# One subtraction of each weight block pair goes from VectorE to GpSimd

## The chip, the cores and the metric

The kernel runs on 1 core of one Trainium2 chip. A core has a matrix engine, TensorE (PE in the profile; PEld is its weight load, which overlaps the matmuls), and three engines that work on tiles: VectorE (DVE), ScalarE (ACT) and GpSimd (POOL). SyncE (SP) issues the transfers from main memory here. Each engine takes its instructions in the program's order and waits for the others by semaphores. Tiles lie in SBUF, the results of matmuls in PSUM. The metric is the device time of one execution, in microseconds.

## The reference

Two layers of a small diffusion transformer work on 256 latent tokens and 256 context tokens of width 1024. Each layer has a swiglu, a mixer (a short convolution in the first layer, attention in the second) and another swiglu, each with a modulated norm ahead of it and a gate behind it:

```python
def _swiglu(h, w13, w2):
    gte, up = jnp.split(h @ w13, 2, axis=-1)
    return (jax.nn.silu(gte) * up) @ w2

for i in range(DEPTH):
    mod = (jax.nn.silu(c) @ mod_w[i] + mod_b[i]).reshape(bsz, 3, 3, 1, D_MODEL)
    lat = lat + 0.5 * mod[:, 0, 2] * _swiglu(_modulate(lat, ...), ffn_w13[i, 0], ffn_w2[i, 0])
    ...   # the same for the context, then the mixer, then the second swiglu
```

The hidden width is 2816, 22 blocks of 128. All of it is computed in float32.

## The kernel before

**Three matmuls for one.** A matmul here takes operands in a shortened form of float32 (F32R). To keep float32's precision, each operand is split into a high part, which is the operand rounded, and a low part, which is what the rounding left. `split` (L91) does that: ScalarE copies with rounding (L92), VectorE subtracts the copy from the source (L93). `mm3` (L112) then issues three matmuls: high by high (L116), high by low of the moving operand (L117), and low of the weight by high (L118). Every weight passes through `split` after it is loaded.

**Seven products for eight.** In most of the swiglus, where latent and context tokens are worked on together, a block of gate weights and its block of up weights are taken as a 2 x 2 arrangement of sub-blocks (A11, A12, A21, A22), and the inputs as another, and the product is formed in seven smaller products rather than eight. The class `Pair` (L525) does it for one of the 22 blocks. Its constructor loads the raw weights, 128 x 2048, forms the sums S1 to S4 on VectorE (L548, L554, L556), and splits A11 with A12, S1 with S2, and S3 with S4, in tiles of 1024 columns named wh and wl, with four buffers of each. A22 is split last, into tiles of 512 columns named w4h and w4l (L558 to L561), with two buffers of each. Raw blocks (wr) have three buffers; the queue of SyncE refills one (L88) when all that read it are done.

**The order within a pair.** The products are `head` (A11, A12), `five` (S1), `six` (S2, S4), `seven` (S3) and `four` (A22). The loop in `ffn` (L600) interleaves two pairs: `head` and `five` of a pair, `seven` of the pair before, `six` of this pair, `four` of the pair before. So A22's high and low parts are read later than any other block of their pair. Between the products VectorE joins sums (L586, L591), multiplies gate and up (L597) and subtracts for the low part of the result (gl, L93).

**Thirds.** A swiglu goes through its 22 blocks in thirds of 8, 7 and 7. After each third, `project` (L454) multiplies what was formed by the third's rows of the second weight matrix (tiles py) and adds it to the residual x (L438). The last two pairs' products are mixed into the beginning of that. The first swiglu starts differently: its first third mostly takes the plain form. The last swiglu works on the latent tokens alone and has no pairs. In all there are 56 pairs.

**What else VectorE does.** The modulation vectors of all layers come from products and sums of VectorE (tiles junk, L136), which are issued in small portions by `tick` during `project`. At the start of a swiglu the norm's steps stand there (t, bl and the sums of L323 to L328).

**What sets the order.** The kernel's text gives the instructions with priorities; a scheduler of the framework puts them in an order for each engine by its own estimates of their lengths. So moving one instruction may change the order of others. GpSimd is not used in the kernel's body.

Of the kernel before, what the change touches and what calls it, by code (L numbers as in the profile page):

```python
# [9 lines left out]
F32 = mybir.dt.float32  # L10
F32R = mybir.dt.float32r
BF16 = mybir.dt.bfloat16
AF = mybir.ActivationFunctionType
ALU = mybir.AluOpType
# [25 lines left out]
def hybrid_kernel(ctx: ExitStack, tc: tile.TileContext, a: dict, out: bass.AP):  # L40
    nc = tc.nc
# [12 lines left out]
    def nm(s):  # L54
        uid[0] += 1
        return f"{s}{uid[0]}"
# [29 lines left out]
    def load_raw(src, n=2048):  # L86
        raw = wp.tile([P, 2048], F32, name=nm("wr"), tag="wr", bufs=3)
        nc.sync.dma_start(raw[:, :n], src)  # L88
        return raw

    def split(hi, lo, src):  # L91
        nc.scalar.activation(out=hi, in_=src, func=AF.Copy)  # L92
        nc.vector.tensor_tensor(out=lo, in0=src, in1=hi.bitcast(F32), op=ALU.subtract)  # L93

    def half():

        return tuple(
            wp.tile([P, 1024], F32R, name=nm(t), tag=t, bufs=4) for t in ("wh", "wl")
        )
# [170 lines left out]
    class Plain:  # L270


        def __init__(self, w=T2):
            self.w, self.n = w, 1024 // w
            self.t = [(hot("hh"), hot("hl")) for _ in range(KT // self.n)]
# [249 lines left out]
    class Pair:  # L525
# [6 lines left out]
        def __init__(self, src, h):  # L532
            self.h = h
            raw = load_raw(src)
            a21, a22, a11, a12 = (raw[:, i * T2 : i * T2 + T2] for i in range(4))
            tt = nc.vector.tensor_tensor
            sm = wp.tile([P, 2048], F32, name=nm("ws"), tag="ws", bufs=1)
            s1, s2, s3, s4 = (sm[:, i * T2 : i * T2 + T2] for i in range(4))
            self.w = {}

            def keep(keys, src):
                hi, lo = half()
                split(hi, lo, src)
                for i, key in enumerate(keys):
                    self.w[key] = [t[:, i * T2 : i * T2 + T2] for t in (hi, lo)]

            keep(("A11", "A12"), raw[:, 1024:])
            tt(  # L548
                out=sm.rearrange("p (a b c) -> p a b c", a=2, b=2)[:, :, 0, :],
                in0=a21.unsqueeze(1).to_broadcast([P, 2, T2]),  # L550
                in1=raw[:, T2 : 3 * T2].rearrange("p (a c) -> p a c", a=2),
                op=ALU.subtract,
            )
            tt(out=s2, in0=a11, in1=s1, op=ALU.subtract)  # L554
            keep(("S1", "S2"), sm[:, :1024])
            tt(out=s4, in0=a12, in1=s2, op=ALU.subtract)  # L556
            keep(("S3", "S4"), sm[:, 1024:])
            self.w["A22"] = [  # L558
                wp.tile([P, T2], F32R, name=nm(t), tag=t, bufs=2) for t in ("w4h", "w4l")
            ]  # L560
            split(*self.w["A22"], a22)  # L561

        def prod(self, ps, wk, hk, first=True):
            for k in range(4):
# [143 lines left out]
    for s in range(2):  # L708
# [6 lines left out]
        out=sb1, in0=modb[:, 0, KT : 2 * KT], scalar1=1.0, scalar2=None, op0=ALU.add  # L715
# [96 lines left out]
    for m in range(KT):  # L812
# [4 lines left out]
        for c0, c1 in ((0, S), (S, T2)) if m == 0 else ((0, T2),):  # L817
# [15 lines left out]
            out=d, in0=u, scalar1=convk[:, 1, m : m + 1], scalar2=None, op0=ALU.mult  # L833
# [4 lines left out]
            out=d2[:, :, 1:], in0=u2[:, :, : S - 1], scalar=convk[:, 0, m : m + 1],  # L838
            in1=d2[:, :, 1:], op0=ALU.mult, op1=ALU.add,
        )  # L840
        nc.vector.scalar_tensor_tensor(
            out=d2[:, :, : S - 1], in0=u2[:, :, 1:], scalar=convk[:, 2, m : m + 1],
            in1=d2[:, :, : S - 1], op0=ALU.mult, op1=ALU.add,
# [151 lines left out]
    for kv in range(KVH):  # L995
# [7 lines left out]
        out=scq, in0=rq[:, :16], scalar1=float(P) ** -0.5, scalar2=None, op0=ALU.mult  # L1003
# [163 lines left out]
```

## Time and profile before

| | us |
|---|---|
| median of 3 runs | 1614.27 |
| lowest and highest | 1613.15, 1616.92 |
| profiled execution | 1611.37 |
| its span | 1609.5 |
| TensorE busy | 1576.1 |
| VectorE busy | 1332.4 |
| ScalarE busy | 722.2 |
| GpSimd busy | 0.2 |
| mean granted TensorE clock | 0.992 of full speed |

The span is from the first instruction's start to the last one's end; the profiled execution took 1.87 us more than its span. Matmuls overlap in their pipeline: a 256-column one is shown with some 283 ns, but the next starts 120 ns after it, so a busy TensorE may still lose time to waits, and starts are what to read. In a row of the timeline come start, length, engine, line, operation and tiles, and in brackets how long the engine stood idle before it and for whom. In a group's row, behind the bar, come busy time in us, mean length in ns, and the idle time before them. A row of waits has the total in us, the number and the longest. The chain of waits is followed back from the last instruction, at each step to what released it.

### The profile page before, as it was taken

To read this page: it belongs to the slowest core of one execution; us is meant where nothing else is said; L and a number is where in the kernel's file an instruction comes from. 1 tells how busy PE (TensorE), PEld (TensorE's weight loads), DVE (VectorE), ACT (ScalarE), POOL (GpSimd) and SP (SyncE) were. 2 spreads that over 40 slices of the span, in tenths; PEclk is the share of its full clock that TensorE was granted. 3 is DMA by queue.
4 is the path that set the end of the run, shared out by engine and by line. 5 is a ranking of instruction groups with operands and counts; after the bars stand their busy time and mean duration, and the time that the engine had idled before them with its cause. 6 is when DMAs were issued, how large, how long until landed. Compare 5 with 4: busy or idle time off the path is not lost.

```text
span 1609.5 us, 25613 instructions
## 1 busy us (share of the span) xinstructions
PE 1576.1 (98%) x10566; PEld 1450.1 (90%) x10566; DVE 1332.4 (83%) x2035; ACT 722.2 (45%) x1110; POOL 0.2 (0%) x4
## 2 busy tenths in 40 slices
PE   9999999999999999999999999999999999899999
PEld 6788998999888889899899889889899897789999
DVE  4988778879998889799797999898898789965554
ACT  5532452544322365335255465245254455454443
POOL 0000000000000000000000000000000000000000
PEclk9999999999999999999999999999999999999999
DMA  8456235234565513353433413452432463755453
GB/s 320 162 183 209 80 122 180 90 135 152 177 221 186 180 41 117 132 183 100 168 120 115 154 54 131 172 195 96 156 129 96 180 214 108 270 201 185 169 194 109
DMA packets 38277, 248.77 MB, mean 155 GB/s; under 512 B 5136, under 2 KB 6928, under 8 KB 12304
## 3 DMA queue, kind: packets, MB, share of 16 engines
q1 hardware_dynamic: 35712, 245.38, 43.7%
q10 hardware_dynamic: 2448, 1.76, 0.4%
q8 instruction: 82, 1.34, 0.3%
q14 instruction: 35, 0.29, 0.1%
HBM read 244.77 MB, written 1.05 MB: 153 GB/s over the span
## 4 chain that ended last, share of the span: by engine, by line
PE 82%; DVE 12%; DMA 3%; ACT 2%; issue 1%; DVEq 0%; ACTq 0%; SPq 0%
PE py L117 7%; PE py L116 7%; PE py L118 7%; PE p L116 6%; PE p L118 6%; PE p L117 6%; PE q L118 5%; PE q L116 5%; PE q L117 5%; DVE junk L136 4%; DVE wl L93 3%; PE pg L117 2%; PE pg L118 2%; PE pg L116 2%; PE pu L117 2%; PE pu L118 2%
## 5 line engine op out<-in xcount | busy, mean ns | idle before, releaser
L92 ACT ACTIVATE wh<-wr 128x1024 fp32r<-128x1024 f32 (+2 forms) x274 | 274.4, 1014 | 395.0 <-PE py L117 108.7
L93 DVE TENSOR_TENSOR wl<-wr,wh 128x1024 fp32r<-128x1024 f32 (+2 forms) x274 | 318.2, 1167 | 97.0 <-ACT wh L92 96.4
L136 DVE CUSTOM_DVE_ANT_0 junk<-wr,scbc,modb 128x1024 bf16<-128x1024 f32 x236 | 302.5, 1282 | 39.6 <-DMA wr<-in_modT 37.0
L117 PE MATMUL py<-gl,wh 128*128 128x512 f32 (+1 forms) x746 | 263.2, 353 | 0.0
L116 PE MATMUL py<-gh,wh 128*128 128x512 f32 (+1 forms) x746 | 263.1, 353 | 0.0
L118 PE MATMUL py<-gh,wl 128*128 128x512 f32 (+1 forms) x746 | 262.9, 352 | 0.0
L93 DVE TENSOR_TENSOR wl<-ws,wh 128x1024 fp32r<-128x1024 f32 x112 | 136.8, 1223 | 27.3 <-ACT wh L92 27.0
L118 PEld LDWEIGHTS py<-gh,wl 128*128 128x128 f32 x746 | 141.1, 189 | 19.1
L116 PEld LDWEIGHTS py<-gh,wh 128*128 128x128 f32 x746 | 141.2, 189 | 18.6
L117 PEld LDWEIGHTS py<-gl,wh 128*128 128x128 f32 x746 | 141.2, 189 | 18.0
L92 ACT ACTIVATE wh<-ws 128x1024 fp32r<-128x1024 f32 x112 | 117.8, 1057 | 76.4 <-PE p L117 34.2
L116 PE MATMUL p<-th,wh 128*128 128x256 f32 x448 | 126.8, 283 | 0.0
L117 PE MATMUL p<-tl,wh 128*128 128x256 f32 x448 | 126.8, 283 | 0.0
L118 PE MATMUL p<-th,wl 128*128 128x256 f32 x448 | 126.6, 283 | 0.0
L117 PE MATMUL q<-bl,wh 128*128 128x256 f32 x336 | 95.2, 283 | 0.0
L116 PE MATMUL q<-bh,wh 128*128 128x256 f32 x336 | 95.1, 283 | 0.0
L118 PE MATMUL q<-bh,wl 128*128 128x256 f32 x336 | 95.1, 283 | 0.0
L438 DVE SCALAR_TENSOR_TENSOR x<-py,G,x 128x256 f32<-128x256 f32 x168 | 74.2, 480 | 21.4 <-PE py L118 21.2
L116 PEld LDWEIGHTS p<-th,wh 128*128 128x128 f32 x448 | 86.0, 192 | 0.5 <-ACT sg L584 0.2
L117 PEld LDWEIGHTS p<-tl,wh 128*128 128x128 f32 x448 | 86.0, 192 | 0.3
L118 PEld LDWEIGHTS p<-th,wl 128*128 128x128 f32 x448 | 85.9, 192 | 0.0
L116 PE MATMUL pg<-hh,wh 128*128 128x256 f32 (+1 forms) x240 | 75.8, 316 | 4.6 <-ACT hh L260 4.6
(236 smaller groups left out, 4001.3 us busy)
## 6 DMA issues: line engine op xcount, KB each, us to landing
wr<-in_w SPq DMA_DIRECT2D x88, 1024.0 KB, 4.9
wr<-in_modT SPq DMA_DIRECT2D x67, 1024.0 KB, 4.9
wr<-in_w2b SPq DMA_DIRECT2D x32, 896.0 KB, 4.6
wr<-in_w2a SPq DMA_DIRECT2D x16, 1024.0 KB, 4.9
wr<-in_cw_cx SPq DMA_DIRECT2D x8, 1024.0 KB, 4.9
wr<-in_mod SPq DMA_DIRECT2D x5, 1024.0 KB, 7.4
wr<-in_cw_b SPq DMA_DIRECT2D x4, 1024.0 KB, 4.8
wr<-in_cw_out SPq DMA_DIRECT2D x4, 1024.0 KB, 4.9
```

Source lines behind the costliest of these rows:

```text
L92: nc.scalar.activation(out=hi, in_=src, func=AF.Copy)
L93: nc.vector.tensor_tensor(out=lo, in0=src, in1=hi.bitcast(F32), op=ALU.subtract)
L116: nc.tensor.matmul(ps, wh, mh, start=first, stop=False, **kw)
L117: nc.tensor.matmul(ps, wh, ml, start=False, stop=False, **kw)
L118: nc.tensor.matmul(ps, wl, mh, start=False, stop=last, **kw)
L136: nc.vector.tensor_tensor_reduce(out=junk, in0=raw[:, j * D : j * D + D], in1=scbc[:, v, :], scale=1.0, scalar=modb[:, l, col : col + 1], ...
L438: nc.vector.scalar_tensor_tensor(out=x[:, m, s * S : s * S + S], in0=ps[:, o : o + S], scalar=g[:, m, s : s + 1], in1=x[:, m, s * S : s * ...
```

## The change

In the constructor of `Pair`, the split of A22 is written out. ScalarE's rounding stays as it was. The subtraction that gives the low part w4l, 128 x 512, is issued to GpSimd instead of VectorE. Operands, tiles and buffers are the same; all 56 pairs are touched.

```diff
             self.w["A22"] = [
                 wp.tile([P, T2], F32R, name=nm(t), tag=t, bufs=2) for t in ("w4h", "w4l")
             ]
-            split(*self.w["A22"], a22)
+
+            hi, lo = self.w["A22"]
+            nc.scalar.activation(out=hi, in_=a22, func=AF.Copy)
+            nc.gpsimd.tensor_tensor(out=lo, in0=a22, in1=hi.bitcast(F32), op=ALU.subtract)
```

## The prediction

> **What bounds the kernel now.** I began with the page's busy times, went on to its chain of waits, and then cut the span into stages, because the change touches only the stages that work on block pairs.
>
> ```profile
> PE 1576.1 (98%) x10566; PEld 1450.1 (90%) x10566; DVE 1332.4 (83%) x2035; ACT 722.2 (45%) x1110; POOL 0.2 (0%) x4
> PE 82%; DVE 12%; DMA 3%; ACT 2%; issue 1%; DVEq 0%; ACTq 0%; SPq 0%
> ```
>
> TensorE (PE) is busy 98% of the span and is 82% of the chain. VectorE (DVE) holds 12% of the chain, GpSimd (POOL) does nothing. So work taken from VectorE can only pay where the chain is VectorE's. The table by stage says where that is (columns: window, its length, busy time and count of PE, PEld, DVE, ACT, POOL, granted clock, share and rate of the transfers):
>
> ```profile
> 187.35:227.67 40.32, 40.32 (x339) 40.32 (x338) 35.04 (x45) 23.49 (x36) 0.00 (x0) 1.00 0.29 99
> 580.00:620.00 40.00, 36.48 (x277) 35.48 (x277) 37.97 (x46) 27.48 (x42) 0.00 (x0) 0.91 0.16 53
> 920.00:950.00 30.00, 26.38 (x185) 25.02 (x185) 26.18 (x42) 19.22 (x36) 0.00 (x0) 0.89 0.13 46
> 950.00:990.00 40.00, 40.00 (x333) 39.82 (x332) 39.05 (x51) 25.78 (x41) 0.00 (x0) 1.00 0.39 132
> 1050.00:1085.00 35.00, 33.42 (x235) 31.09 (x234) 34.89 (x50) 15.71 (x24) 0.00 (x0) 1.00 0.58 201
> ```
>
> The first row is four pairs in steady state: TensorE has no gap. A pair is 84 matmuls, 40.32 / 4 = 10.08 us, 0.120 us a matmul. VectorE works 35.04 / 4 = 8.76 us of each 10.08 and has 1.32 us free. The other four rows are the tight places: the starts of the second and third pair-form swiglus (580 and 920), the first pairs after 950, and the start of the third's second part (1050). There VectorE is 87 to 99.7% busy and TensorE loses time. In two of them the granted clock falls to 0.91 and 0.89, which is 0.09 x 40 = 3.6 us and 0.11 x 30 = 3.3 us of clock.
>
> **The change, part by part.** The moved subtraction, with the ScalarE (ACT) rounding that feeds it:
>
> ```profile
> L93 DVE TENSOR_TENSOR w4l<-wr,w4h 128x512 fp32r<-128x512 f32 x56 | 38.4, 687 | 0.0
> ...
> L92 ACT ACTIVATE w4h<-wr 128x512 fp32r<-128x512 f32 x56 | 35.1, 627 | 59.9 <-PE p L117 43.3 <-DMA wr<-in_w 16.5
> ```
>
> *Removed from VectorE:* 56 subtractions of 0.687 us. Back to back a 512-column one takes 0.60 us of the queue (in the timeline below the next starts 0.60 us later), so 56 x 0.60 = 33.6 us of queue. About 47 of them lie in steady stages, behind TensorE's 10.08 us a pair: worth 0.
>
> *Added to GpSimd:* 56 subtractions and, in the program's order, one code-load instruction ahead of the first. The queue held only four memsets of 0.10 us, so nothing is passed or held up there. No row shows a GpSimd subtraction. Lower end: ScalarE's copy of the same shape, 0.63 us. Upper end: twice VectorE's, 1.37 us. I take the upper end, as nothing in the trace shows this engine keeping up with the others. Its length matters little by itself: lining the trace up with the program's order, w4l ends 14.1 us or more before the first matmul that reads it, in all 56. The code load stands about 150 us ahead of the first subtraction (158.6), which itself has 27.4 us to spare; were it charged there, 25 us would still be covered.
>
> *The wait on the raw block.* The load that refills the raw buffer often waits for this subtraction:
>
> ```profile
> 187.99 0.63 ACT L92 ACTIVATE w4h<-wr 128x512 fp32r<-128x512 f32 x1 [1.56 <-PE p L117]
> 189.08 0.68 DVE L597 TENSOR_TENSOR gm<-sg,p 128x512 f32<-128x512 f32 x1
> 189.68 0.69 DVE L93 TENSOR_TENSOR w4l<-wr,w4h 128x512 fp32r<-128x512 f32 x1
> 190.28 0.69 DVE L554 TENSOR_TENSOR ws<-wr,ws 128x512 f32<-128x512 f32 x1
> 190.39 10.41 SPq L88 DMA_DIRECT2D wr<-in_w  x2
> ```
>
> ```profile
> SPq L88 <- DVE w4l L93: 404.7, 41, 24.9
> ```
>
> w4h is ready at 188.62, but w4l stands in VectorE's queue until 189.68; the load goes out at 190.39. GpSimd can start at 188.62 and end at 188.62 + 1.37 = 189.99, so SP's queue, in order, moves on 0.4 us earlier, not later. The load takes 4.9 us and is used more than a pair later. Taken at 0; were GpSimd 1 us late, 41 loads would be late by that under the same cover.
>
> *What GpSimd does to VectorE.* Both would read SBUF at once, and no row shows what that costs. Lower end 0: both run undisturbed, and VectorE gains its 0.60 us. Upper end: VectorE stands for the whole subtraction, 1.37 us, and loses 1.37 - 0.60 = 0.77 us for each. In a steady pair either end is covered: 0.77 is less than the 1.32 us free, and wl blocks there end a median 5 us before use. I take the middle, +0.085 us.
>
> The Trainium skill (SBUF — State Buffer, Who interferes with whom) speaks against the change: a VectorE instruction with two SBUF inputs and a GpSimd instruction that reads SBUF use one shared interface, and the second to issue waits for the first to finish. The same skill (GPSIMD Engine Reference, Performance versus the Vector engine) gives 4497 ns for 2048 columns, as an estimate 1.12 us for 512; a full hold by that figure would cost 0.52 us net each, and the sum below would be +4.7 instead of +0.8 us. No run here shows it yet.
>
> *The tight places.* Nine roundings w4h start there (607, 916, 923, 963, 973, 983, 1057, 1063, 1080), and their subtractions follow at once. Here is the clearest one, from the chain in order of time:
>
> ```profile
> 1061.34 0.60 DVE ws L554
> 1061.94 0.60 DVE w4l L93
> 1062.54 0.60 DVE ws L556
> 1063.14 1.20 DVE junk L136
> 1064.34 0.01 DVE mod L136
> 1064.35 1.15 DVE wl L93
> 1065.49 0.04 issue
> 1065.54 0.39 PE q L118
> ```
>
> w4l is on the chain, and TensorE waits 1.30 us for the wl behind it. Of the wl blocks after 950 and 1060, six end less than 0.7 us before their use, so a delay passes on to TensorE. Nine times -0.60 to +0.77 is -5.4 to +6.9 us; nine times the middle is +0.8 us.
>
> *What the scheduler moves.* SP's order is unchanged. In the steady pairs, s4 (L556) simply closes up, as w4l leaves. At the third swiglu's start, two of the modulation products (1.28 us each) that stood at 970.6 and 973.2 are now queued between the norm's VectorE steps near 920 to 931, which delays that chain by up to 2.4 us; the 1.22 us wl that TensorE waits for until 929.6 moves ahead of it, which takes up to 2.2 us of wait away. Taken as even, 0, bounds -2.2 to +2.4.
>
> **Sum.** 0 (steady) + 0 (loads) + 0.8 (tight places) + 0 (order) = +0.8 us. The profiled execution took 1611.37: span 1609.5 and 1.87 around it. So one like it would take 1612.2. The median of three, 1614.27, is 2.9 above the profiled one; from it the forecast is 1615.1. A measurement of this kernel can tell about 0.2%, 3.2 us, from no change.
>
> **Rivals.**
>
> *Slower: VectorE held in the tight places.* If GpSimd holds VectorE for the upper end, nine times 0.77 is 6.9 us; some of it is absorbed, but a longer stand at 1064 can bring the clock fall that 580 and 920 show (3.3 to 3.6 us) and that this place now escapes (1.00). +4 to +9, say 1620. For it: margins of 0.05 to 0.36 us. Against: few subtractions lie there. It decides from a hold of about 1.1 us net of cover (nine times 0.5 passes 3.2 us).
>
> *Much slower: the pairs become VectorE's.* It needs a hold above 1.32 + 0.60 = 1.92 us for each subtraction, all the time. At 2.9 us it costs about 1 us in 47 pairs: 1661. For it: no row of this engine at work. Against: it is 1.4 times my upper end.
>
> *Faster: the freed time reaches TensorE.* If GpSimd doesn't disturb, the 1.30 us wait at 1065 falls by 0.60 to 1.2, the start at 920 loses its 2.2 us wait and perhaps part of its 3.3 us of clock: -3.5 to -5.5, about 1610. For it: VectorE at 99.7% in that row. Against: at 580 TensorE's 3 us wait is for ScalarE's bh, which no w4l precedes closely.
>
> That the change does not do what it says can be left out: the program's order has 56 subtractions on POOL and none of w4l on DVE.
>
> **How the numbers follow.** About no change 0.45; slower in the tight places 0.28; much slower 0.05; faster 0.22. So faster 0.22, same 0.45, slower 0.33. The likeliest case alone spans 1611.1 to 1617.5. The range reaches down into the faster case (1609.3) and up through the tight-place case (1623), leaving out about 1 in 10 on each side.
>
> **What would show it.** Right: 56 w4l rows on POOL of 0.6 to 1.4 us; VectorE's busy time down by some 34 us, or less if its own rows grow; steady windows without a TensorE gap; loads waiting for POOL at the same times. The hold shows as VectorE's two-input rows stretched, or gaps before them, beside a POOL row. Wrong: POOL rows of 2 us or more, gaps in TensorE in steady pairs, or a granted clock below 1 in a window where it was 1.

## The result, and the profile after

The changed kernel takes 1620.48 us (median of 7 runs, 1619.01 to 1624.52), the kernel before 1614.27 (7 runs beside them, 1612.65 to 1617.38). The ratio is 1.0039, 95% interval 1.0025 to 1.0053: 6.2 us slower. The prediction said 1615.1, with a range of 1609.3 to 1623.0. The range holds the time because it had been drawn up to the tight-place rival; the likeliest case, no change, is not what happened. Its rival "VectorE held in the tight places" is, at almost its price (1620).

The profiled execution of the changed kernel took 1619.96 us, with a span of 1618.2. The page's busy times and its chain of waits, after:

```profile
PE 1580.1 (98%) x10566; PEld 1450.6 (90%) x10566; DVE 1333.2 (82%) x1979; ACT 723.5 (45%) x1110; POOL 90.3 (6%) x60
PE 79%; DVE 14%; DMA 3%; issue 2%; ACT 1%; ACTq 0%; SPq 0%; DVEq 0%
```

VectorE has 56 instructions fewer (1979 against 2035) and is no less busy: 1333.2 against 1332.4 us. Its share of the chain has not fallen but grown, from 12% to 14%. What it was relieved of has come back as longer instructions. The groups by form show which (busy time in us, mean in ns, idle time before them). Before:

```profile
L556 DVE TENSOR_TENSOR ws<-wr,ws 128x512 f32<-128x512 f32 x56 | 38.5, 688 | 0.4
L554 DVE TENSOR_TENSOR ws<-wr,ws 128x512 f32<-128x512 f32 x56 | 38.5, 687 | 0.3
```

After:

```profile
L564 POOL TENSOR_TENSOR w4l<-wr,w4h 128x512 fp32r<-128x512 f32 x56 | 90.1, 1610 | 1149.6 <-ACT w4h L563 1149.6
...
L554 DVE TENSOR_TENSOR ws<-wr,ws 128x512 f32<-128x512 f32 x56 | 53.2, 949 | 0.3
...
L556 DVE TENSOR_TENSOR ws<-wr,ws 128x512 f32<-128x512 f32 x56 | 38.5, 688 | 1.3
```

GpSimd takes 1.61 us on average for what VectorE did in 0.687. The sum at L554 took 687 ns before and takes 949 now; its twin at L556, with the same shape and operands, is as before. L554 is the one that stands beside GpSimd's subtraction in most steady pairs. It is longer in 27 of the 56 pairs; the rest of VectorE's lost time lies in gl, L548, wl and junk where they stand there. A steady pair in the timeline shows it. First GpSimd's row, then VectorE's (start, length, engine, line, operation, tiles):

```profile
192.07 1.56 POOL L564 TENSOR_TENSOR w4l<-wr,w4h 128x512 fp32r<-128x512 f32 x1 [29.66 <-ACT w4h L563]
```

```profile
192.39 0.68 DVE L600 TENSOR_TENSOR gm<-sg,p 128x512 f32<-128x512 f32 x1
192.99 1.19 DVE L554 TENSOR_TENSOR ws<-wr,ws 128x512 f32<-128x512 f32 x1
194.21 0.69 DVE L556 TENSOR_TENSOR ws<-wr,ws 128x512 f32<-128x512 f32 x1
```

GpSimd works from 192.07 to 193.63. The product gm, one of whose operands (p) lies in PSUM, passes beside it in its usual 0.68 us. L554, whose operands both lie in SBUF, takes 1.19 instead of 0.69: it starts at 192.99, and counted from GpSimd's end at 193.63 the rest is 0.55 us, close to the 0.60 that an undisturbed one takes of the queue. So it is held until GpSimd is done, and not slowed throughout.

The same stages as before the prediction, in the changed kernel (window, length, busy time and count of PE, PEld, DVE, ACT and POOL, granted clock, share and rate of the transfers; the steady row is taken 4.65 us later and again takes in four pairs):

```profile
192.00:232.32 40.32, 40.32 (x338) 40.32 (x338) 34.92 (x41) 23.48 (x37) 6.24 (x4) 1.00 0.30 99
580.00:620.00 40.00, 36.03 (x268) 34.75 (x267) 35.28 (x42) 24.54 (x37) 1.30 (x1) 0.91 0.18 64
920.00:950.00 30.00, 25.69 (x189) 24.13 (x187) 27.25 (x46) 19.95 (x39) 3.10 (x2) 0.94 0.31 112
950.00:990.00 40.00, 38.37 (x311) 37.49 (x311) 39.22 (x44) 26.12 (x38) 4.04 (x2) 1.00 0.23 80
1050.00:1085.00 35.00, 32.42 (x193) 28.34 (x192) 34.89 (x49) 12.31 (x17) 3.61 (x2) 1.00 0.55 199
```

In the steady row TensorE has no gap, as before. The other rows cannot be subtracted from the old ones line by line, because the later stages have shifted (by 7.1 us in the last row, where one and the same L548 starts at 1065.31 instead of 1058.20). Of these, 3.3 us stood already at 81 us, before any w4l: there one and the same matmul starts at 84.41 instead of 81.11. The profiles of the ten experiments are 1.0 to 4.3 us late at that matmul, those without any work of GpSimd's among them, so this part belongs to the single execution and not to the change. The rows do show where GpSimd meets a nearly full VectorE: 39.22 of 40 us from 950, 34.89 of 35 from 1050.

At the start of a third the hold looks different. VectorE's timeline at the place that the prediction called the clearest one, and GpSimd's two subtractions there:

```profile
1065.31 1.22 DVE L548 TENSOR_TENSOR ws<-wr 128x1024 f32<-128x1024 f32 x1
1066.44 2.31 DVE L93 TENSOR_TENSOR wl<-wr,wh 128x1024 fp32r<-128x1024 f32 x1
...
1071.87 1.21 DVE L93 TENSOR_TENSOR wl<-ws,wh 128x1024 fp32r<-128x1024 f32 x1
1073.01 2.31 DVE L136 CUSTOM_DVE_ANT_0 junk<-wr,scbc,modb 128x1024 bf16<-128x1024 f32 x1
...
1075.25 1.22 DVE L93 TENSOR_TENSOR wl<-ws,wh 128x1024 fp32r<-128x1024 f32 x1
```

```profile
1066.06 1.61 POOL L564 TENSOR_TENSOR w4l<-wr,w4h 128x512 fp32r<-128x512 f32 x1 [53.44 <-ACT w4h L563]
...
1072.24 2.00 POOL L564 TENSOR_TENSOR w4l<-wr,w4h 128x512 fp32r<-128x512 f32 x1 [4.57 <-ACT w4h L563]
```

Here a wl of 1024 columns takes 2.31 us instead of 1.22, and a modulation product 2.31 instead of 1.28. Each is held for more than 1 us, and nothing without a second SBUF operand stands between. It goes the other way too: the second subtraction starts at 1072.24, beside the wl that runs until 1073.08, and takes 2.00 us.

### The profile page after: what moved, and what is told of

Read it like the earlier page. It is cut to its first block, busy times and chain, and to the rows that moved or that the text cites. A ratio compares the mean times of both kernels' runs of the same rounds, so it can differ in the third digit from the quotient of the medians.

```text
span 1618.2 us, 25755 instructions
## 1 busy us (share of the span) xinstructions
PE 1580.1 (98%) x10566; PEld 1450.6 (90%) x10566; DVE 1333.2 (82%) x1979; ACT 723.5 (45%) x1110; POOL 90.3 (6%) x60
## 4 chain that ended last, share of the span: by engine, by line
PE 79%; DVE 14%; DMA 3%; issue 2%; ACT 1%; ACTq 0%; SPq 0%; DVEq 0%
PE py L116 7%; PE py L117 7%; PE py L118 7%; PE p L118 6%; PE p L116 6%; PE p L117 6%; PE q L118 5%; PE q L116 5%; PE q L117 5%; DVE junk L136 4%; DVE wl L93 3%; PE pg L117 2%; PE pg L118 2%; PE pg L116 2%; PE pu L118 2%; PE pu L117 2%
## 5 line engine op out<-in xcount | busy, mean ns | idle before, releaser
L93 DVE TENSOR_TENSOR wl<-wr,wh 128x1024 fp32r<-128x1024 f32 (+2 forms) x274 | 323.3, 1186 | 97.3 <-ACT wh L92 96.8
L564 POOL TENSOR_TENSOR w4l<-wr,w4h 128x512 fp32r<-128x512 f32 x56 | 90.1, 1610 | 1149.6 <-ACT w4h L563 1149.6
```

The lines of the kernel that those rows point to most:

```text
L564: nc.gpsimd.tensor_tensor(out=lo, in0=a22, in1=hi.bitcast(F32), op=ALU.subtract)
```

## The experiments

The theory after the result: GpSimd's subtraction holds VectorE's instructions with two SBUF operands; in steady pairs this is covered, and at the starts of the thirds it delays TensorE. The rivals: the code that GpSimd loads before its first subtraction disturbs the start; the scheduler's new order of VectorE's work costs the time; the hold costs a little in every pair. The pairs can be parted by place: 14 lie in the first thirds of swiglus, 12 are the first two of each later third, and the other 30 are steady.

Four runs made on one chip beside the kernel before (median 1614.31, 23 runs) part the change into code load, order and hold.

**The code load alone.** The kernel before, with one tiny GpSimd subtraction ahead of the work:

```diff
+    once = const.tile([P, 1], F32, name="once", tag="once")
+    nc.gpsimd.tensor_tensor(out=once, in0=eps_t, in1=eps_t, op=ALU.subtract)
```

> The kernel before, with one GpSimd subtraction of 128x1 added early on, so that the code-load instruction stands at the front of GpSimd's queue; PE, DVE, ACT and SP keep the order of before. In the changed kernel's profile TensorE is 3.3 us late by 81 us, before any w4l exists. Theory 'code load': that loss is the load's, so this kernel takes about 3 us more than before (1617) and its in_mod blocks land late as in the profile after. Theory 'scatter of the first transfers': no change (1614), and the start looks as before.

Measured: 1614.61 (11 runs), ratio 1.0001 [0.9993, 1.0010]. The load and a first use cost nothing that shows; no row of the profile shows the load itself.

**The code load moved.** The changed kernel, with one more small GpSimd instruction in front, so that the load comes about 65 us into the execution:

```diff
+    nc.gpsimd.memset(ris[0][:, :1], 0.0)
```

> The changed kernel, with one GpSimd memset of 128x1 on a tile that is free at about 60 us, ahead of the code load, so that the load leaves the start; all other engines keep the changed kernel's order. Theory 'code load': 3 us faster than the changed kernel (1617). Theory 'scatter': as the changed kernel (1620.5).

Measured: 1621.06 (6 runs), ratio 1.0045 [1.0032, 1.0058], as slow as the changed kernel. With the run above, the code load is out.

**The relief and the order without the hold.** No low part of A22 is formed at all; the matmuls that read it read the high part. VectorE and TensorE have the same order of instructions as in the changed kernel:

```diff
-            split(*self.w["A22"], a22)
+            hi = self.w["A22"][0]
+            nc.scalar.activation(out=hi, in_=a22, func=AF.Copy)
+            self.w["A22"] = [hi, hi]
```

> The low part of A22 is not computed at all; its matmuls read the high part in its place. VectorE and TensorE have the changed kernel's order, without GpSimd. Theory 'GpSimd holds VectorE': the loss after 81 us (5.3 us in the profiles) is gone, and with VectorE relieved of 56 subtractions the time is at or below before: 1610 to 1614. Theory 'the new order costs': still 3 to 5 us above before, 1617 to 1619.

Measured: 1613.76 (12 runs), ratio 0.9997 [0.9987, 1.0006]. The page of its profiled execution, which at 1618.6 is the slowest of its 12:

```profile
PE 1581.0 (98%) x10566; PEld 1453.7 (90%) x10566; DVE 1304.9 (81%) x1979; ACT 724.0 (45%) x1110; POOL 0.2 (0%) x4
```

VectorE is 27.5 us less busy than before (1304.9 against 1332.4), and the kernel is not measurably faster: relief and new order together change the time by -0.5 us (-2.1 to +1.0). So these two do not make the 6 us. The changed kernel has the same instructions on VectorE and 28.3 us more of busy time there (1333.2): 0.51 us for each of GpSimd's 56 subtractions. The time between this kernel and the one above it, on the same chip and in the same order on TensorE and VectorE, is 1621.06 - 1613.76 = 7.3 us; against the changed kernel's own median it is 6.7. That is the price of the hold.

VectorE's timeline in this kernel, at the same place as above:

```profile
1062.66 1.22 DVE L548 TENSOR_TENSOR ws<-wr 128x1024 f32<-128x1024 f32 x1
1063.80 1.22 DVE L93 TENSOR_TENSOR wl<-wr,wh 128x1024 fp32r<-128x1024 f32 x1
...
1068.13 1.22 DVE L93 TENSOR_TENSOR wl<-ws,wh 128x1024 fp32r<-128x1024 f32 x1
1069.27 1.28 DVE L136 CUSTOM_DVE_ANT_0 junk<-wr,scbc,modb 128x1024 bf16<-128x1024 f32 x1
...
1070.47 1.22 DVE L93 TENSOR_TENSOR wl<-ws,wh 128x1024 fp32r<-128x1024 f32 x1
```

The same instructions stand in the same order, and none is held. From the start of L548 to the end of the wl (of S1 and S2) that TensorE waits for next it takes 1069.35 - 1062.66 = 6.69 us here and 1073.08 - 1065.31 = 7.77 in the changed kernel: a hold of 1.08 us by one subtraction. Before the change it was 1065.49 - 1058.20 = 7.29, with w4l itself in between. So at this place the relief of 0.60 and the hold of 1.08 make a net loss of 0.48 us. By the next wl the second subtraction has held the product ahead of it: it ends 9.03 us after L548's start here and 11.16 in the changed kernel, 2.13 us later.

**The hold without the relief.** The kernel before, with VectorE doing its own subtraction as ever, and GpSimd doing the same once more into a tile that nobody reads. The order on the four other queues is that of before:

```diff
             split(*self.w["A22"], a22)
+            w4x = wp.tile([P, T2], F32R, name=nm("w4x"), tag="w4x", bufs=1)
+            nc.gpsimd.tensor_tensor(
+                out=w4x, in0=a22, in1=self.w["A22"][0].bitcast(F32), op=ALU.subtract
+            )
```

> The kernel before, VectorE keeping its subtraction, and GpSimd computing the same low part once more into a tile that nobody reads. The order of PE, DVE, ACT and SP is that of before. Theory 'GpSimd holds VectorE': the hold without the relief, so more than the changed kernel after 81 us: +6 to +10 us, with the start's 3.3 us 1623 to 1628. Theory 'the new order costs': only the start's 3.3 us, 1617.5, or nothing if that is scatter.

Measured: 1626.27 (5 runs), ratio 1.0073 [1.0061, 1.0085], 12.0 us slower. VectorE's busy time and the group that now stands beside GpSimd:

```profile
PE 1583.1 (97%) x10566; PEld 1452.1 (89%) x10566; DVE 1369.4 (84%) x2035; ACT 722.0 (44%) x1110; POOL 93.1 (6%) x60
```

```profile
L93 DVE TENSOR_TENSOR w4l<-wr,w4h 128x512 fp32r<-128x512 f32 x56 | 54.5, 974 | 0.0
```

VectorE has the same 2035 instructions as before and is 37.0 us busier, 0.66 for each subtraction of GpSimd's; its own w4l went from 687 to 974 ns. The hold needs neither the new order nor a consumer of GpSimd's result. Without the relief the hold costs 12.0 us, with it 6 to 7. So the relief, with the new order that comes with it, is worth 5 to 6 us where VectorE is held, and 0.5 (between -1.0 and 2.1) where it is not. That fits an engine that before the change was just in time in many places; which places of this kernel make up the 12 us was not parted.

Four runs on another chip (kernel before 1614.77, 29 runs) ask where it costs, and by what.

**The steady pairs alone, and all the others alone.** GpSimd subtracts in 30 pairs, VectorE in the rest; then the reverse:

```diff
+            eng = nc.gpsimd if gps else nc.vector
+            eng.tensor_tensor(out=lo, in0=a22, in1=hi.bitcast(F32), op=ALU.subtract)
...
-                        pr = Pair(a["w13"][l, b, i0 + i], h)
+                        pr = Pair(a["w13"][l, b, i0 + i], h, t > 0 and i > 1)
```

> GpSimd takes the subtraction only in the 30 pairs that are third or later in a swiglu's second or third third; in the other 26 VectorE keeps it. Theory 'the hold counts only where wl is just in time': no change against before, 1613 to 1616, though GpSimd's rows are as long as in the changed kernel and VectorE's s2 (L554) rows are stretched by 0.5 us. Theory 'every hold costs a little': half of the loss, 1617.

The reverse:

```diff
-                        heads.append(Pair(a["w13"][l, b, i], h))
+                        heads.append(Pair(a["w13"][l, b, i], h, True))
...
-                        pr = Pair(a["w13"][l, b, i0 + i], h)
+                        pr = Pair(a["w13"][l, b, i0 + i], h, not (t > 0 and i > 1))
```

> The complement: GpSimd takes it in the other 26 pairs (the first two of each second or third third, and the whole first thirds), VectorE in the 30. Theory 'just in time': all of the changed kernel's loss, 1619 to 1621. Theory 'every hold costs a little': half, 1617.

Measured: steady pairs 1614.46 (11 runs), ratio 1.0001 [0.9992, 1.0010]; the others 1620.17 (6 runs), 1.0040 [1.0024, 1.0056]. As far as these intervals tell, the whole loss lies in the 26 others. A window of five steady pairs in the first of these kernels, and the group of its held sums:

```profile
186.00:236.00 50.00, 50.00 (x419) 50.00 (x418) 41.13 (x47) 29.11 (x45) 7.66 (x5) 1.00 0.27 92
```

```profile
L554 DVE TENSOR_TENSOR ws<-wr,ws 128x512 f32<-128x512 f32 x56 | 48.1, 859 | 0.3
```

L554 is held here as well: 859 ns against 687 on average over all 56, of which only 30 stand beside GpSimd. TensorE has no gap in the 50 us. So the hold is there in the steady pairs and is covered, and the rival that charges every pair falls.

**A GpSimd instruction that only writes.** The kernel before, with GpSimd setting a tile of 128 x 512 to zero once in each pair, started by the same rounding (through a copy of one column, which is all that it reads):

```diff
+            w4x = wp.tile([P, T2], F32R, name=nm("w4x"), tag="w4x", bufs=1)
+            nc.gpsimd.tensor_copy(w4x[:, :1], self.w["A22"][0][:, :1].bitcast(F32))
+            nc.gpsimd.memset(w4x.bitcast(F32), 0.0)
```

> As the run in which GpSimd repeats the subtraction, but GpSimd reads only one column of w4h (so that it starts at the same moment) and then writes 512 columns without reading. Order of the other engines as before. Theory 'the reads collide': VectorE's rows keep their lengths and the time is that of before, 1614. Theory 'any GpSimd access to SBUF holds VectorE': rows next to the memset are stretched by up to its length, and the time lies between before and 1626.

Measured: 1614.49 (10 runs), ratio 1.0000 [0.9991, 1.0009]. GpSimd's row, and VectorE's at that moment:

```profile
612.34 0.53 POOL L564 MEMSET w4x<- 128x512 f32 x1
```

```profile
612.36 0.69 DVE L554 TENSOR_TENSOR ws<-wr,ws 128x512 f32<-128x512 f32 x1
```

The zeroing runs from 612.34 to 612.87. L554, with two SBUF operands, starts 0.02 us later and takes its usual 0.69. In most other pairs the two overlap less, but of 59 instructions with SBUF operands alone that stand beside a zeroing none is longer than usual by more than 0.01 us, and VectorE's busy time is 1333.1 against 1332.4. So neither GpSimd's being at work nor its writing holds VectorE; what is left is its reading.

**The subtraction later in the text, on VectorE.** No GpSimd; the kernel's text splits A22 only when `six` begins, behind the wl blocks:

```diff
+        def last_split(self):
...
-            split(*self.w["A22"], a22)
+            split(*self.w["A22"], self.a22)
...
+            self.last_split()
```

> No GpSimd. The whole split of A22 stays on ScalarE and VectorE and is issued later, in the method six, so that it no longer stands ahead of s4 and the wl that TensorE waits for at 1065. Theory 'the w4l on that chain costs its 0.60 us': 0 to 1.5 us below before, 1613 to 1614. Rival: the raw block is freed later and a load lands late, 1615 to 1618.

Measured: 1615.38 (11 runs), ratio 1.0005 [0.9995, 1.0016]. That is not told from no change, and it is above the 1613 to 1614 that the theory expected. But the run does not test the theory. The scheduler put the subtraction back: in VectorE's order of this profile it has the same two neighbours as before in 55 of the 56 pairs, at the clearest place too:

```profile
1063.03 0.68 DVE L554 TENSOR_TENSOR ws<-wr,ws 128x512 f32<-128x512 f32 x1
1063.62 0.69 DVE L93 TENSOR_TENSOR w4l<-wr,w4h 128x512 fp32r<-128x512 f32 x1
1064.23 0.69 DVE L556 TENSOR_TENSOR ws<-wr,ws 128x512 f32<-128x512 f32 x1
```

So TensorE's wait for wl in the window from 1055 to 1095 us is the one of before:

```profile
PE q L118 <- DVE wl L93: 1.3, 1, 1.3
```

What w4l costs at this place is told by the kernel without it alone, where that wait is 0.7 us. The rival of this run, a load that lands late, stays untested as well.

Two runs on a third chip (kernel before 1614.71, 23 runs) part the 26 pairs.

**The first two pairs of the later thirds; the first thirds.** As above, with other selections; the first kernel has 12 pairs on GpSimd:

```diff
-                        pr = Pair(a["w13"][l, b, i0 + i], h)
+                        pr = Pair(a["w13"][l, b, i0 + i], h, t > 0 and i < 2)
```

The second has 14:

```diff
-                        heads.append(Pair(a["w13"][l, b, i], h))
+                        heads.append(Pair(a["w13"][l, b, i], h, True))
...
-                        pr = Pair(a["w13"][l, b, i0 + i], h)
+                        pr = Pair(a["w13"][l, b, i0 + i], h, t == 0)
```

> GpSimd takes the subtraction in 12 pairs alone: the first two of each second or third third. In the profiles of the changed kernel and of its twin with the late code load, TensorE loses 1.5 to 2.1 us at 719, 1.3 to 2.2 at 1065 to 1085 and 0.7 to 0.9 at 1185 against the kernel without the low part, 3.5 to 5 us in all. Theory 'these three places carry it': +3.5 to +5 us over before, 1618 to 1619.5. Rival 'the first thirds carry it': within 1 us of before.

> GpSimd takes the subtraction in the 14 pairs of the two first thirds alone (the starts at 580 and 920 and the pairs behind them). Theory 'the second and third thirds' starts carry it': 0 to +2 us, 1614 to 1616.5. Rival 'the first thirds carry it': +5 to +6 us, 1619.5 to 1620.5.

Measured: the 12 pairs 1617.78 (12 runs), ratio 1.0020 [1.0008, 1.0032], so +3.2 us (1.3 to 5.2), 0.27 a pair; the 14 pairs 1615.68 (12 runs), 1.0010 [0.9999, 1.0021], so +1.6 us (-0.2 to 3.4), which is not told from zero. The two together make 4.8, and the run with all 26 showed 6.5 with an interval of 3.9 to 9.0: they add up as far as these intervals can tell. The first is a little below the 1618 to 1619.5 that its theory expected from losses near 719, 1065 and 1185; in this kernel's profile, counted at the same matmuls as before, TensorE loses 1.8 us between 700 and 760, 1.7 between 1060 and 1100, and 0.1 between 1160 and 1200. The larger share seems to lie in the 12 pairs that follow a `project`, where VectorE has the modulation products, the residual's sums and the new pair's blocks to do at once; the two intervals overlap, so this order is likely and not shown.

## Why the prediction was right and wrong

**The steady pairs at 0: right.** 30 pairs on GpSimd cost +0.2 us (-1.3 to +1.6), though the hold was there. The 1.32 us that VectorE has free in a pair covers it, as the prediction argued.

**The loads at 0: right.** SP's queue waits for the new subtraction about as often as for the old one, and for less time (total, number, longest):

```profile
SPq L88 <- POOL w4l L564: 244.7, 39, 7.1
```

Before it was 404.7 us in 41 waits. All its waits at L88 together are as long as before (1505 us against 1497), since other readers of the raw block now come last. What counts is that no load comes later: the rounding w4h waits 14.0 us for loads of raw blocks, before 16.5.

**The code load at 0: right.** Both runs on it show nothing.

**GpSimd's length: the upper end was too low, without effect.** The prediction bounded it by 1.37 us. The tile's view in the changed kernel (min, median, max in ns):

```profile
L564 POOL TENSOR_TENSOR w4l<-wr,w4h x56: 1289/1560/2361, 156.8 to 1238.9; 128x512 fp32r<-128x512 f32 x56
```

Undisturbed it is 1.29 us, but its mean is 1.61, because it also waits for VectorE. Seven rows take 2.0 us or more, which the prediction had named as a sign of being wrong; its range of 0.6 to 1.4 us for a row left out that wait. TensorE never waits for w4l, since the matmuls read it 14 us later or more; ScalarE waits for its buffer once, 1.6 us.

**The size of the hold: the middle was good for the mean and wrong for the place.** The prediction took +0.085 us net, a hold of 0.685. The mean is 0.51 in the changed kernel and 0.66 with VectorE's own subtraction kept. But the mean is drawn down by gm, which isn't held and happens to stand beside GpSimd's row in 29 of the 30 steady pairs and in only 9 of the 26 others.

**The tight places at +0.8: the step that failed.** The prediction took nine times the middle of its two ends, a hold of 0.685 us and a net loss of 0.085. At its clearest place the profile shows a hold of 1.08 us at 1066 and 1.03 at 1073 (a product of 2.31 instead of 1.28), about midway between that middle and the upper end of 1.37; against the relief of 0.60 the first is a net loss of 0.48 us. There VectorE does two-operand work back to back, and nothing with a PSUM operand stands beside GpSimd. Nine times 0.48 would have been 4.3 us instead of 0.8. The count of nine was too small besides: the loss lies in the 26 pairs outside the steady stages, 6.5 us in all, 0.25 a pair (which of them lose was not run one by one). The list left out five of the six starts of later thirds, which had no gap in TensorE before and hence did not look tight. Not all of them lose: at the same matmuls the profile of the changed kernel falls behind by 1.5 us between 700 and 760 and by 0.7 between 1160 and 1200, but not near 157, 272 and 810. The window from 700 to 740 us, before and after:

```profile
700.00:740.00 40.00, 40.00 (x319) 39.26 (x319) 39.24 (x53) 22.54 (x34) 0.00 (x0) 1.00 0.40 142
```

```profile
700.00:740.00 40.00, 38.98 (x289) 37.10 (x288) 38.91 (x48) 20.62 (x31) 5.96 (x4) 1.00 0.39 132
```

Before, VectorE was 39.24 of 40 us busy with TensorE just kept supplied; now TensorE loses 1.02 us. Its waits in that window, of which there were none without the hold, are:

```profile
PE q L118 <- DVE wl L93: 0.8, 1, 0.8
PE q L116 <- ACT wh L92: 0.2, 1, 0.2
```

The prediction's sentence that TensorE loses time in all four tight rows was wrong in the same sense: the row from 950 to 990 had 40.00 of 40. In these two rows VectorE's share, 98%, said more than whether TensorE already waited.

**The order at 0: about 1 us short at one place.** Relief and new order together gave -0.5 us, and no run parts their times. The profiles show the order at the start of the third swiglu, where the prediction had set bounds of -2.2 to +2.4 us. In the window from 915 to 990 us TensorE's waits add up to 4.2 us before and to 5.2 in the kernel without the low part, where GpSimd does nothing; in the changed kernel it is 5.7. The row that grows most, before and in the kernel without the low part:

```profile
PE pg L116 <- ACT bh L92: 0.6, 1, 0.6
```

```profile
PE pg L116 <- ACT bh L92: 2.5, 2, 1.4
```

All five profiles with the new order at this place have 5.2 to 6.3 us of such waits, the seven others 3.8 to 4.5. So a part of what the 14 pairs of the first thirds seem to cost is the new order and not the hold.

**The rivals.** The slower one happened, by its mechanism. That its price of 1620 was met is in part luck: its holds were too long (1.37 us against 1.08 and 1.03) and its places too few, and the clock fall that it feared near 1064 did not come (granted clock 1.00 from 1050 to 1085; it fell to 0.97 from 1063 to 1113 in the profile of the kernel with the 14 pairs, where nothing held VectorE). Its point of decision, a hold of 1.1 us, which less the relief of 0.60 is the 0.5 of its bracket, was well set: the holds at 1066 and 1073 come to it within 0.1 us. The faster one is excluded further than by the result alone. Even with no hold at all the relief gives -0.5 us. In that kernel's profile TensorE's wait for wl in this window does fall from 1.3 to 0.7 us, as the rival had it, yet the whole is not faster: the 1.0 us more of waits from 915 to 990 is the likely place where it is given back, which these single profiles suggest and do not prove. Much slower is excluded by the steady pairs.

**The rule on the shared interface.** The Trainium skill (SBUF — State Buffer, Who interferes with whom) says that a VectorE instruction with two SBUF inputs contends with a GpSimd instruction that reads SBUF, and not with one that only writes. The runs agree on each point: beside GpSimd's subtraction L554 is held by 0.5 us, gm with its operand in PSUM is not, and beside a GpSimd zeroing L554 takes its usual 0.69 us. The sum that the prediction gave by this rule, +4.7, was nearer to the measured 6.2 than the +0.8 that it chose, though it counts the same nine places.

## What to carry to other kernels

Before work is moved from VectorE to GpSimd, look at which VectorE instructions will stand beside it: here those with two SBUF operands waited until GpSimd's subtraction was done, and the move gave back in busy time all that it freed (28.3 us against 27.5). Price it at the places where VectorE is nearly full, with the instructions that stand there, and not with the average over the kernel; a place where TensorE doesn't wait yet, but VectorE is at 98%, is such a place. To see whether an engine's relief can be worth anything, leave the work out once: here that run left at most 2.1 us to win, by its interval. And read the built order before a run that moves an instruction is believed: here the scheduler put a moved subtraction back in 55 of 56 places.

## What the runs showed of the hardware

- A 512-column float32 subtraction on GpSimd takes 1.29 us undisturbed, 1.9 times VectorE's 0.687, and up to 2.36 us where an instruction of VectorE with SBUF operands alone has begun before it: the hold goes both ways.
- The custom modulation product of VectorE (junk, 1.28 us) is held as a plain subtraction is: 2.31 us.
- Zeroing 128 x 512 on GpSimd takes 0.53 us. A copy of a single column takes 0.18 us where it isn't held and 0.52 on average, for example 1.02 beside a wl of VectorE: even a read of one column waits.
- GpSimd's code load, once and ahead of the first use, cost nothing that shows (ratio 1.0001 [0.9993, 1.0010]).
